# Hyena filters: output layer in two float32r passes, its input stored by step

## The chip, the cores and the metric

The kernel runs on one core of one Trainium2 chip. The metric is the device time of one launch in microseconds, as the median of several runs. The core's engines work at the same time, each through its own instruction stream in order: TensorE (PE in the profile, with its weight loads as PEld), VectorE (DVE), ScalarE (ACT), GpSimd (POOL) and SyncE (SP, which here issues nearly all DMAs).

## The reference

One encoder layer on a sequence of 2048 rows of width 1024: an input projection, a Hyena group of 512 channels beside an mLSTM group, an output projection, cross-attention, an MLP and a final norm. What the change touches is how the Hyena filters are made:

```python
def _hyena_filter_spectrum(L, w1, b1, fr1, w2, b2, fr2, w3):
    ...
    hid = jnp.sin(fr1.astype(f32) * (z @ w1.astype(f32) + b1.astype(f32)))
    hid = jnp.sin(fr2.astype(f32) * (hid @ w2.astype(f32) + b2.astype(f32)))
    filt = (hid @ w3.astype(f32)).reshape(L, HYENA_ORDER, FILTER_DIRS, D_HYENA)
    ...
    filt = filt * jnp.exp(-t * jnp.abs(deltas))[:, None, None, :]
    fwd = filt[:, :, 0]
    bwd = jnp.flip(filt[1:, :, 1], axis=0)
    two_sided = jnp.concatenate([fwd, jnp.zeros((1, HYENA_ORDER, D_HYENA), f32), bwd], axis=0)
    return jnp.fft.rfft(two_sided, axis=0)
```

There are two orders (`o`), two directions (`r`: forward, backward), 64 hidden features and 512 channels. "The output layer" is `hid @ w3`.

## The kernel before

The program is written as Python generators that yield the weight of the work they have just put down; `weave(a, b, wa, wb)` (L1594) takes turns between two of them in proportion to the weights. A scheduler then orders the instructions of each engine ahead of time by a simulated timeline, with the order of the program as priority, and adds the semaphores; tiles of one tag share a fixed number of buffers, and an instruction that needs a buffer waits until it is free.

The first stage weaves `filters()` (L158) with `sweep()` (L500), which multiplies the input projection. Each `sweep` step is 24 matmuls of `mm3` (L294 to L297): a float32 product made of three passes over operands that were cut into a high and a low part of type float32r (`split`, L299: ScalarE writes the rounded high part, VectorE subtracts to get the low one). A float32r matmul is one pass. The filters' own matmuls (L208, L212, L238, L253, L254, L284) are plain float32, each two records in the trace.

`filters()` has three parts.

- L202 to L213, four chunks of 512 positions: features, two small matmuls and two `sine` calls (L189 to L199). Both directions are computed at once, forward features on rows 0 to 63, backward ones on rows 64 to 127. The result is `hid`, 128 rows by 2048 positions.
- L244 to L264, the output loop, eight steps `j2` of two position classes `j` each (all positions congruent to `j` modulo 16) and two orders: the forward taps are a matmul of rows 0 to 63 of `hid[.., j::16]` with rows 0 to 63 of `w3` (L253), the backward taps one of rows 64 to 127 (L254). VectorE multiplies both by the decay windows (L256, L257, loaded at L224), adds them into `e[0]` (L261), GpSimd subtracts them into `e[1]` (L262). One round later (`late`) the two products with the first Fourier stage `f1` follow (L238, "fronts"), ScalarE copies them into `st` (L239), and SP stores them to the DRAM tensors `fs0` and `fs1` (L241).
- L266 to L286, 32 "blocks": load `dm` and a piece of `fs` (L268, L270), two matmuls (L284), two copies (L285), store to the DRAM tensor `hd` (L286).

All this lives in one pool, `f_sb`, with seven buffers `a` of 4 KB per partition and eight `b` of 2 KB; PSUM tiles `hy` have four banks, `mm` of the sweeps another four.

`hyena()` (L626) follows, woven with the rest of the sweeps and the natural-order products (`natural`, L593). Its middle loop (i from 0 to 15, for each order) loads per step `dm` and `em` (128 KB each), `t` from `zs` (512 KB), and four pieces of `hd` of 256 KB (L663, L664), each of 64 partitions, as the real and imaginary rows go to both halves of the partitions; it stores 512 KB to `zg`.

Of the kernel before, what the change touches and what calls it, by code (L numbers as in the profile page):

```python
# [18 lines left out]
L = 2048  # L19
D = 1024  # L20
CH = 512
# [6 lines left out]
def shape_constants():  # L28
# [39 lines left out]
    dm = np.zeros((32, 2, 64, 2, 64))  # L68
# [29 lines left out]
class Prog:  # L98
# [59 lines left out]
    def filters(self):  # L158
        nc, tc, a = self.nc, self.tc, self.a
        sd = [self.dram(f"fs{o}", (2, 128, 16, CH)) for o in range(2)]  # L160
        hd = self.dram("hd", (2, 32, 128, CH))
        with tc.tile_pool(name="f_sb", bufs=1, side="right") as sb:
            def ta(bufs=7):
                return sb.tile([128, 2, CH], F32, tag="a", name="a", bufs=bufs)

            def tb(bufs=8):
                return sb.tile([128, CH], F32, tag="b", name="b", bufs=bufs)

            w1 = sb.tile([66, 128], F32, name="w1")
            w2 = sb.tile([128, 128], F32, name="w2")  # L170
            w3 = sb.tile([128, 2, CH], F32, name="w3")
            f1 = sb.tile([128, 2, 128], F32, name="f1")
            nc.vector.memset(w1, 0.0)
            nc.vector.memset(w2, 0.0)
            nc.gpsimd.dma_start(out=w1[0:33, 0:64], in_=a["hy_filt_w1"][0])
            nc.gpsimd.dma_start(out=w1[33:66, 64:128], in_=a["hy_filt_w1"][0])
            nc.gpsimd.dma_start(out=w2[0:64, 0:64], in_=a["hy_filt_w2"][0])
# [37 lines left out]
            skip, skip2 = tb(), tb()  # L215
            for o, t in enumerate((skip, skip2)):
                nc.scalar.dma_start(out=t[0:1], in_=a["hy_skip"][:, o])
            wv = a["c_win"].rearrange("r (q j) c -> r q j c", j=16)
            def windows(j2):
                if j2 == 8:  # L220
                    return None
                w = ta(), ta()
                for r in range(2):
                    nc.sync.dma_start(out=w[r], in_=wv[r, :, 2 * j2:2 * j2 + 2])  # L224
                return w

            held = []
# [1 line left out]
            def late(f):  # L229
                if held:  # L230
                    held.pop()()
                if f is not None:
                    held.append(f)
# [7 lines left out]
                        nc.sync.dma_start(out=sd[o][p, :, js], in_=st[p])  # L241

            nxt = windows(0)
            for j2 in range(8):  # L244
                js = slice(2 * j2, 2 * j2 + 2)
                yield 14
                (wf, wb), nxt = nxt, windows(j2 + 1)
                for o in range(2):
                    st = [ta() for p in range(2)]
                    for jj in range(2):  # L250
                        j = 2 * j2 + jj
                        pf, pb = self.hy(), self.hy()
                        nc.tensor.matmul(pf, hid[0:64, j::16], w3[0:64, o], start=True, stop=True)  # L253
                        nc.tensor.matmul(pb, hid[64:128, j::16], w3[64:128, o], start=True, stop=True)  # L254
                        f, b = tb(), tb()
                        nc.vector.tensor_tensor(f, pf, wf[:, jj], ALU.mult)  # L256
                        nc.vector.tensor_tensor(b, pb, wb[:, jj], ALU.mult)  # L257
                        if j == 0:
                            nc.vector.tensor_tensor(f[0:1], f[0:1], (skip, skip2)[o][0:1], ALU.add)
                        e = [tb() for p in range(2)]  # L260
                        nc.vector.tensor_tensor(e[0], f, b, ALU.add)  # L261
                        nc.gpsimd.tensor_tensor(e[1], f, b, ALU.subtract)  # L262
                        late(lambda e=e, st=st, jj=jj, o=o, js=js: front(e, st, jj, o, js))
            late(None)  # L264
            def blocks(o, i):
                p, k = divmod(2 * i, 16)  # L266
                dm = sb.tile([128, 2, 128], F32, tag="dm", name="dm", bufs=3)
                nc.sync.dma_start(out=dm, in_=a["c_dm"][:, 2 * i:2 * i + 2])  # L268
                t = ta()
                nc.sync.dma_start(out=t, in_=sd[o][p, 8 * k:8 * k + 16].rearrange("(k r) j c -> (r j) k c", k=2))  # L270
                return dm, t

            order = [(o, i) for o in range(2) for i in range(16)]
            q = [blocks(*order[0]), blocks(*order[1])]
            for n, (o, i) in enumerate(order):
                if True:
                    yield 3.4
                    dm, t = q.pop(0)
                    if n + 2 < 32:
                        q.append(blocks(*order[n + 2]))  # L280
                    hs = ta()
                    for m in range(2):
                        pp = self.hy()
                        nc.tensor.matmul(pp, dm[:, m], t[:, m], start=True, stop=True)  # L284
                        nc.scalar.copy(hs[:, m], pp)  # L285
# [307 lines left out]
    def natural(self, hf, tiles, after=None):  # L593
        nc, a, sb = self.nc, self.a, self.isb
        xh, xl = self.xh, self.xl
        win = a["w_in"][0]
        for c2 in tiles:
            n = 256 if c2 < 3 else 272
            c0 = 2560 + 256 * c2
            wh, wl = next(self.wst)  # L600
            for t in range(8):
                if t % 4 == 0:
                    yield 11
                if t == 4 and c2 == tiles[-1] and after is not None:
                    after()
                ts = slice(128 * t, 128 * t + 128)
                r0 = 1024 * hf + 128 * t
                p = self.mm()
                for k in range(8):
                    self.mm3(p[:, :n], xh[:, k, ts], xl[:, k, ts], wh[:, k, :n], wl[:, k, :n], k == 0, k == 7)  # L610
                if self.pending:
                    self.pending.pop(0)()
                self.pop()
                so = sb.tile([128, 256], F32, tag="so", name="so", bufs=3)
                if c2 < 2:
                    nc.scalar.copy(so, p[:, :256])
                else:
                    nc.scalar.activation(so, p[:, :256], AF.Sigmoid)
                nc.sync.dma_start(out=(self.d_vd if c2 < 2 else self.d_od)[r0:r0 + 128, 256 * (c2 % 2):256 * (c2 % 2) + 256],
                                  in_=so)  # L620
                if c2 == 3:
                    sg = sb.tile([128, 16], F32, tag="sg", name="sg", bufs=2)
                    nc.vector.tensor_tensor(sg, p[:, 256:272], self.gb, ALU.add)
                    nc.sync.dma_start(out=self.d_gt[r0:r0 + 128], in_=sg)

    def hyena(self, es):  # L626
        nc, tc, a = self.nc, self.tc, self.a
        hy = self.dram("hy", (3, L, CH)).rearrange("s (q j) c -> s q j c", j=16)
        hd = self.dram("hd", (2, 32, 128, CH))
# [23 lines left out]
        def load2(o, i):  # L653
# [4 lines left out]
            nc.sync.dma_start(out=em, in_=a["c_em"][:, 2 * i:2 * i + 2])  # L658
            t, hr, hi = ta(), ta(), ta()
            nc.sync.dma_start(out=t, in_=sds[o][p, 8 * k:8 * k + 16].rearrange("(k r) j c -> (r j) k c", k=2))  # L660
            src = hd[o, 2 * i:2 * i + 2].rearrange("k (r l) c -> r l k c", r=2)
            for h in range(2):
                nc.sync.dma_start(out=hr[64 * h:64 * h + 64], in_=src[0])  # L663
                nc.sync.dma_start(out=hi[64 * h:64 * h + 64], in_=src[1])  # L664
            if i == 0:
                nc.sync.dma_start(out=hr[64:65, 0], in_=hd[o, 0, 64:65])
# [28 lines left out]
        for o in range(2):  # L695
# [16 lines left out]
            nxt = load2(o, 0)  # L712
# [899 lines left out]
def program(p):  # L1612
    with ExitStack() as ms:
        with ExitStack() as es:
# [61 lines left out]
```

## Time and profile before

| | us |
|---|---|
| median of 3 runs | 3396.99 (3387.59 to 3401.57) |
| the profiled execution | 3389.34 |
| its span | 3387.6 |
| filters' sine chunks | up to 112 |
| filters' output loop | 112 to 304 |
| filters' blocks | 304 to 463 |
| Hyena (order 0 middle loop: 520 to 720) | from 475 |

The mean granted clock of TensorE in this execution was 0.978 of full speed. In the profile a line gives engine, operation, tiles (written <- read) and shape; "idle before" is the time in which that engine stood still ahead of these instructions, with what ended it. Ends of matmuls are modelled, so that a record's length holds its passage through the array: matmuls that follow each other overlap in the records, and their cost is the distance from start to start.

### The profile page before, as it was taken

What the parts mean: (1) busy time and instruction counts of PE and PEld (TensorE: products, weight loads), DVE (VectorE), ACT (ScalarE), POOL (GpSimd) and SP (SyncE); (2) the same over time, 40 slices, a digit from 0 to 9 for tenths busy, and PEclk for the clock granted to TensorE, in tenths of its full rate; (3) what the DMA queues carried; (4) which work ended last, traced back from release to release, by engine and by line L of the source; (5) the groups of instructions that cost most, each with busy time, mean ns of one, the idle gap of its engine ahead of it and who ended that gap; (6) DMA issues with size and microseconds to landing.
All of it is one profiled execution on the core that took longest, in us unless ns stands there. A gap on an engine that the chain in (4) does not pass through costs nothing.

```text
span 3387.6 us, 46777 instructions
## 1 busy us (share of the span) xinstructions
PE 3200.0 (94%) x15671; PEld 2560.6 (76%) x15671; DVE 2084.2 (62%) x3855; ACT 1459.1 (43%) x2771; POOL 1227.3 (36%) x862
## 2 busy tenths in 40 slices
PE   6999999899899988799999999999999999999997
PEld 5656666577676877688897987788788887888876
DVE  7584324443556757787776554765854576556695
ACT  4344434442554233344344444555655543333335
POOL 2131001210122312333325012876766564434482
PEclk9999999899999989899999999999999999999998
DMA  5356888996999578856547444765654475444424
GB/s 164 115 205 206 277 288 232 258 322 254 253 242 296 178 236 277 256 162 215 187 152 265 144 134 155 224 206 184 199 171 157 148 242 174 128 140 140 128 94 159
DMA packets 480750, 674.55 MB, mean 199 GB/s; under 512 B 41739, under 2 KB 256849, under 8 KB 479485
## 3 DMA queue, kind: packets, MB, share of 16 engines
q1 hardware_dynamic: 478904, 668.70, 62.4%
q0 software_dynamic: 1600, 2.86, 0.3%
q8 instruction: 124, 2.03, 0.2%
q14 instruction: 118, 0.96, 0.1%
q10 hardware_dynamic: 4, 0.00, 0.0%
HBM read 452.23 MB, written 219.18 MB: 198 GB/s over the span
## 4 chain that ended last, share of the span: by engine, by line
PE 47%; DVE 7%; DMA 6%; issue 2%; ACT 1%; POOL 1%; SPq 0%; DVEq 0%; ACTq 0%; POOLq 0%
PE mm L297 10%; PE mm L295 10%; PE mm L296 10%; PE hy L297 5%; PE hy L296 5%; PE hy L295 5%; DVE rw L945 1%; DVE wl L301 1%; DMA rw<-rows 1%; DMA wr<-xs 1%; DVE bl L1266 1%; PE hy L1092 1%; DMA wn<-in_xa_wq_dram 1%; DMA wr<-in_ff_w_dram 0%; PE hy L972 0%
## 5 line engine op out<-in xcount | busy, mean ns | idle before, releaser
L301 DVE TENSOR_TENSOR wl<-wn,wh 128x512 fp32r<-128x512 f32 (+1 forms) x352 | 263.1, 778 | 135.0 <-ACT wh L300 134.4
L295 PE MATMUL mm<-xh,wh 128*128 128x512 f32 (+1 forms) x768 | 316.7, 413 | 10.9 <-ACT P L530 9.3
L1266 DVE TENSOR_TENSOR bl<-wr,bh 128x512 fp32r<-128x512 f32 x213 | 237.0, 1118 | 133.2 <-ACT bh L1265 131.2
L297 PE MATMUL mm<-xh,wl 128*128 128x512 f32 (+1 forms) x768 | 302.8, 395 | 3.3 <-DVE wl L301 3.3
L1265 ACT CAST ah<-w 128x512 fp32r<-128x512 f32 x284 | 176.2, 622 | 299.9 <-PE hy L296 153.7
L296 PE MATMUL mm<-xl,wh 128*128 128x512 f32 (+1 forms) x768 | 303.7, 396 | 0.2 <-DVE xr_y L150 0.2
L300 ACT CAST wh<-wn 128x512 fp32r<-128x512 f32 (+1 forms) x352 | 202.0, 618 | 229.9 <-PE mm L296 77.1
L727 POOL TENSOR_TENSOR b<-b,a 128x512 f32<-128x512 f32 x64 | 91.9, 1438 | 498.1 <-ACT b L725 201.1
L1266 DVE TENSOR_TENSOR al<-w,ah 128x512 fp32r<-128x512 f32 x236 | 224.4, 952 | 56.8 <-ACT ah L1265 56.5
L1265 ACT CAST bh<-wr 128x512 fp32r<-128x512 f32 x232 | 143.5, 621 | 241.6 <-PE mm L297 171.1
L297 PE MATMUL mm<-bh,al 128*128 128x512 f32 x576 | 225.5, 394 | 6.6 <-DVE al L1266 3.8
L295 PE MATMUL mm<-bh,ah 128*128 128x512 f32 x576 | 227.1, 394 | 0.3 <-DVE u L1391 0.2
L296 PE MATMUL mm<-bl,ah 128*128 128x512 f32 x576 | 225.8, 392 | 0.0
L295 PE MATMUL mm<-act,wh 128*128 128x512 f32 x512 | 202.0, 398 | 6.2 <-ACT wh L300 6.2
L296 PE MATMUL mm<-act,wh 128*128 128x512 f32 x512 | 202.6, 396 | 0.0
L297 PE MATMUL mm<-act,wl 128*128 128x512 f32 x512 | 201.1, 397 | 0.0
L295 PEld LDWEIGHTS mm<-xh,wh 128*128 128x128 f32 x768 | 148.2, 193 | 60.0 <-issue 18.2
L1131 POOL TENSOR_TENSOR ssum<-ssum,sq 128x512 f32<-128x512 f32 x56 | 81.3, 1451 | 284.7 <-ACT sq L1130 283.9
L297 PEld LDWEIGHTS mm<-xh,wl 128*128 128x128 f32 x768 | 147.8, 192 | 46.3 <-issue 15.8
L296 PEld LDWEIGHTS mm<-xl,wh 128*128 128x128 f32 x768 | 147.9, 193 | 45.5 <-issue 20.0
L295 PE MATMUL hy<-bh,ah 128*128 128x512 f32 x448 | 175.2, 391 | 0.0
L296 PE MATMUL hy<-bl,ah 128*128 128x512 f32 x448 | 174.6, 390 | 0.0
(373 smaller groups left out, 8911.9 us busy)
## 6 DMA issues: line engine op xcount, KB each, us to landing
wr<-hc SPq DMA_DIRECT2D x224, 256.0 KB
w<-in_ff_w_dram SPq DMA_DIRECT2D x176, 256.0 KB
a<-hd SPq DMA_DIRECT2D x128, 256.0 KB
hc<-t SPq DMA_DIRECT2D x128, 256.0 KB
wn<-in_w_in_dram SPq DMA_DIRECT2D x104, 256.0 KB
hc<-q SPq DMA_DIRECT2D x96, 256.0 KB
fs<-a SPq DMA_DIRECT2D x32, 512.0 KB
a<-fs SPq DMA_DIRECT2D x32, 512.0 KB
```

The costliest lines, as they stand in the source:

```text
L295: mm(ps, lh, rh, start=start, stop=False)
L296: mm(ps, lh, rl, start=False, stop=False)
L297: mm(ps, ll, rh, start=False, stop=stop)
L300: self.nc.scalar.copy(hi, src)
L301: self.nc.vector.tensor_tensor(lo, src, hi.bitcast(F32), ALU.subtract)
L727: nc.gpsimd.tensor_tensor(xt, xt, hi[:, m], ALU.mult)
L945: nc.vector.scalar_tensor_tensor(nm[:, h], nm[:, h], GC[:, r + h:r + h + 1], masks[d], ALU.add, ALU.min)
L1092: nc.tensor.transpose(pt[:, 128 * k:128 * k + 128], yn[:, 128 * k:128 * k + 128], self.ident)
L1131: nc.gpsimd.tensor_tensor(ssum, ssum, sq, ALU.add)
L1265: self.nc.scalar.copy(hi, src)
L1266: eng.tensor_tensor(lo, src, hi.bitcast(F32), ALU.subtract)
```

## The change

The output layer becomes float32r. `hid` is written twice, by step: `hid0` holds the high part of the forward rows on partitions 0 to 63 and their low part on 64 to 127; `hid1` the backward rows' high part on 64 to 127 and their low part on 0 to 63. `wide[r]` holds the high part of `w3[r]` on both halves, `wl` the low part (forward on 0 to 63, backward on 64 to 127). Per step, order and direction a matmul of 128 rows gives (high + low) x high, and one of 64 rows adds high x low into the same bank. The stationary operand `hid[r][:, j]` is now contiguous. Windows come one step `j` at a time with both directions in one load. The subtraction overwrites `b`. The blocks get a pool of their own, `f_sb2`. `hd` is laid out so that a row of both frequencies is contiguous, in its stores and loads. `so` of `natural` now uses the tag `st`, which the sweeps' transposed outputs and the norm's scratch also use. The weights of `weave` and the yields change (14 per two steps to 5.3 per step; 230 to 202).

```diff
-    c_win = np.stack([win, winb], 0)
+    c_win = np.stack([win.reshape(128, 16, CH), winb.reshape(128, 16, CH)], 2)
...
-        hd = self.dram("hd", (2, 32, 128, CH))
+        hd = self.dram("hd", (2, 16, 128, 2, CH))
...
-            def ta(bufs=7):
-                return sb.tile([128, 2, CH], F32, tag="a", name="a", bufs=bufs)
-
-            def tb(bufs=8):
-                return sb.tile([128, CH], F32, tag="b", name="b", bufs=bufs)
...
+            def ta():
+                return sb.tile([128, 2, CH], F32, tag="a", name="a", bufs=6)
+
+            def tb():
+                return sb.tile([128, CH], F32, tag="b", name="b", bufs=6)
+
+            ws = ta()
+            w1, w2 = ws[0:66, 0, 0:128], ws[:, 1, 0:128]
...
-            for h in range(2):
-                nc.gpsimd.dma_start(out=w3[64 * h:64 * h + 64], in_=w3v[h])
+            top, low = slice(0, 64), slice(64, 128)
+            raws = [ta() for r in range(2)]
+            for r in range(2):
+                for half in (top, low):
+                    nc.gpsimd.dma_start(out=raws[r][half], in_=w3v[r])
+            wide = [sb.tile([128, 2, CH], F32R, name=f"w3h{r}") for r in range(2)]
+            wl = sb.tile([128, 2, CH], F32R, name="w3l")
...
-            hid = sb.tile([128, L], F32, name="hid")
+            hid = [sb.tile([128, 16, 128], F32R, name=f"hid{r}") for r in range(2)]
...
-                sine(hid[:, cs], p2, 2, 3)
...
+                out = tb()
+                sine(out, p2, 2, 3)
+                src = out.rearrange("p (q j) -> p j q", j=16)
+                qs = slice(32 * c, 32 * c + 32)
+                for r, (own, other) in enumerate(((top, low), (low, top))):
+                    nc.scalar.copy(hid[r][own, :, qs], src[own])
+                    nc.vector.tensor_tensor(src[own], src[own], hid[r][own, :, qs].bitcast(F32), ALU.subtract)
+                    nc.scalar.copy(hid[r][other, :, qs], src[own])
+            for r, own in enumerate((top, low)):
+                for o in range(2):
+                    tc.keep_in_program_order(nc.scalar.copy(wide[r][:, o], raws[r][:, o]))
+                    nc.vector.tensor_tensor(wl[own, o], raws[r][own, o], wide[r][own, o].bitcast(F32), ALU.subtract)
...
+            for j in range(16):
+                jj = j % 2
+                js = slice(j - jj, j - jj + 2)
+                yield 5.3
+                cur, nxt = nxt, windows(j + 1)
+                if jj == 0:
+                    st = [[ta() for p in range(2)] for o in range(2)]
                 for o in range(2):
...
+                    taps = []
+                    for r, own in enumerate((top, low)):
+                        p = self.hy()
+                        nc.tensor.matmul(p, hid[r][:, j], wide[r][:, o], start=True, stop=False)
+                        nc.tensor.matmul(p, hid[r][own, j], wl[own, o], start=False, stop=True)
+                        t = tb()
+                        nc.vector.tensor_tensor(t, p, cur[:, r], ALU.mult)
+                        taps.append(t)
+                    f, b = taps
+                    if j == 0:
+                        skip = tb()
+                        nc.scalar.dma_start(out=skip[0:1], in_=a["hy_skip"][:, o])
+                        nc.vector.tensor_tensor(f[0:1], f[0:1], skip[0:1], ALU.add)
+                    e = tb()
+                    nc.vector.tensor_tensor(e, f, b, ALU.add)
+                    nc.gpsimd.tensor_tensor(b, f, b, ALU.subtract)
+                    late(lambda e=(e, b), st=st[o], jj=jj, o=o, js=js: front(e, st, jj, o, js))
             late(None)
+        with tc.tile_pool(name="f_sb2", bufs=1, side="right") as sb:
...
-                    nc.sync.dma_start(out=hd[o, 2 * i:2 * i + 2].rearrange("k l c -> l k c"), in_=hs)
+                nc.sync.dma_start(out=hd[o, i], in_=hs)
...
-                so = sb.tile([128, 256], F32, tag="so", name="so", bufs=3)
+                so = sb.tile([128, 512], F32, tag="st", name="st", bufs=3)[:, 0:256]
...
-            src = hd[o, 2 * i:2 * i + 2].rearrange("k (r l) c -> r l k c", r=2)
+            src = hd[o, i].rearrange("(r l) k c -> r l k c", r=2)
...
-            weave(p.filters(), s, 230, 200)
+            weave(p.filters(), s, 202, 200)
```

More of the change, by code (lines that the diff above doesn't have):

```diff
@@ L160, in filters @@
         sd = [self.dram(f"fs{o}", (2, 128, 16, CH)) for o in range(2)]
-        hd = self.dram("hd", (2, 32, 128, CH))
+        hd = self.dram("hd", (2, 16, 128, 2, CH))
         with tc.tile_pool(name="f_sb", bufs=1, side="right") as sb:
-            def ta(bufs=7):
-                return sb.tile([128, 2, CH], F32, tag="a", name="a", bufs=bufs)
-            def tb(bufs=8):
-                return sb.tile([128, CH], F32, tag="b", name="b", bufs=bufs)
-            w1 = sb.tile([66, 128], F32, name="w1")
-            w2 = sb.tile([128, 128], F32, name="w2")
-            w3 = sb.tile([128, 2, CH], F32, name="w3")
+            def ta():
[4 more added lines that the diff above has]
+            w1, w2 = ws[0:66, 0, 0:128], ws[:, 1, 0:128]
             f1 = sb.tile([128, 2, 128], F32, name="f1")
-            nc.vector.memset(w1, 0.0)
-            nc.vector.memset(w2, 0.0)
+            nc.vector.memset(ws[:, :, 0:128], 0.0)
             nc.gpsimd.dma_start(out=w1[0:33, 0:64], in_=a["hy_filt_w1"][0])
@@ L212, in filters, with windows @@
                 nc.tensor.matmul(p2, w2, hid1, start=True, stop=True)
-                sine(hid[:, cs], p2, 2, 3)
[L215 to L220, printed above, removed]
-                    return None
-                w = ta(), ta()
-                for r in range(2):
-                    nc.sync.dma_start(out=w[r], in_=wv[r, :, 2 * j2:2 * j2 + 2])
+                out = tb()
[10 more added lines that the diff above has]
+                    nc.vector.tensor_tensor(wl[own, o], raws[r][own, o], wide[r][own, o].bitcast(F32), ALU.subtract)
+            def windows(j):
+                if j == 16:
+                    return None
+                w = ta()
+                nc.sync.dma_start(out=w, in_=a["c_win"][:, j])
                 return w
@@ L243, in filters @@
             nxt = windows(0)
[L244 to L247, printed above, removed]
-                for o in range(2):
[L249 to L263, printed above, removed]
@@ new lines, in filters @@
+            st = None
+            for j in range(16):
[5 more added lines that the diff above has]
+                    st = [[ta() for p in range(2)] for o in range(2)]
+                for o in range(2):
+                    taps = []
[15 more added lines that the diff above has]
+                    late(lambda e=(e, b), st=st[o], jj=jj, o=o, js=js: front(e, st, jj, o, js))
@@ L268, in blocks @@
                 nc.sync.dma_start(out=dm, in_=a["c_dm"][:, 2 * i:2 * i + 2])
-                t = ta()
+                t = sb.tile([128, 2, CH], F32, tag="a", name="a", bufs=8)
                 nc.sync.dma_start(out=t, in_=sd[o][p, 8 * k:8 * k + 16].rearrange("(k r) j c -> (r j) k c", k=2))
@@ L275, in filters @@
             for n, (o, i) in enumerate(order):
[L276 to L285, printed above, removed]
-                    nc.sync.dma_start(out=hd[o, 2 * i:2 * i + 2].rearrange("k l c -> l k c"), in_=hs)
+                yield 3.4
+                dm, t = q.pop(0)
+                if n + 2 < 32:
+                    q.append(blocks(*order[n + 2]))
+                hs = sb.tile([128, 2, CH], F32, tag="a", name="a", bufs=8)
+                for m in range(2):
+                    pp = self.hy()
+                    nc.tensor.matmul(pp, dm[:, m], t[:, m], start=True, stop=True)
+                    nc.scalar.copy(hs[:, m], pp)
+                nc.sync.dma_start(out=hd[o, i], in_=hs)
     def column(self, ap, n, name):
@@ L628, in hyena @@
         hy = self.dram("hy", (3, L, CH)).rearrange("s (q j) c -> s q j c", j=16)
-        hd = self.dram("hd", (2, 32, 128, CH))
+        hd = self.dram("hd", (2, 16, 128, 2, CH))
         yh = self.dram("yh", (L, CH)).rearrange("(q j) c -> q j c", j=16)
@@ L665, in load2 @@
             if i == 0:
-                nc.sync.dma_start(out=hr[64:65, 0], in_=hd[o, 0, 64:65])
+                nc.sync.dma_start(out=hr[64:65, 0], in_=hd[o, 0, 64:65, 0])
                 nc.vector.memset(hi[0:1, 0], 0.0)
```

## The prediction, made before the changed kernel ran

> **What bounds the kernel now.** I read the page's totals first, then the busy time by stage, then the order of instructions on TensorE inside the stage that the change rewrites.
>
> ```profile
> span 3387.6 us, 46777 instructions
> PE 3200.0 (94%) x15671; PEld 2560.6 (76%) x15671; DVE 2084.2 (62%) x3855; ACT 1459.1 (43%) x2771; POOL 1227.3 (36%) x862
> ```
>
> ```profile
> 20.00:47.00 27.00, 17.07 (x64) 12.85 (x65) 22.49 (x83) 14.23 (x30) 2.81 (x5) 0.96 0.80 251
> ...
> 112.00:304.00 192.00, 190.19 (x650) 109.33 (x649) 137.50 (x273) 77.37 (x147) 56.71 (x31) 1.00 0.49 169
> ...
> 463.00:475.00 12.00, 10.28 (x51) 8.41 (x50) 5.29 (x8) 5.01 (x8) 0.59 (x1) 1.00 0.69 227
> ```
>
> A row of the windows gives its length, then busy time of PE, PEld, DVE, ACT and POOL, the granted clock, the DMA share and GB/s. The filters' output loop runs from 112 to 304 us: TensorE is busy 190.2 of 192 us at full clock, DVE 137.5. So in that stage time is TensorE time, and the question is how much of it the old output layer takes. Its matmuls are L253 and L254, which read `hid` on rows 0–63 and 64–127. The first row below is both lines together, the second L254 alone (windows from 0 to 304 us).
>
> ```profile
> sum 304.00, PE 56.27 PEld 24.55 ACT 2.53; mean PE 11.25 PEld 4.91 ACT 0.51
> ```
>
> ```profile
> sum 304.00, PE 38.94 PEld 16.42; mean PE 7.79 PEld 3.28
> ```
>
> Two times 38.94 is 77.9, yet together they keep TensorE busy for only 56.3 us: 21.6 us of it two matmuls ran at once. One float32 matmul of 64 rows is two records, 1.23 us; 21.6 / 1.23 makes some 18 of the 32 pairs that run side by side, and 14 that don't. The timeline shows one of each.
>
> ```profile
> 205.21 0.40 PE L295 MATMUL mm<-xh,wh 128*128 128x512 f32 x1
> ...
> 205.45 0.40 PE L296 MATMUL mm<-xl,wh 128*128 128x512 f32 x1
> 205.77 0.29 PEld L253 LDWEIGHTS hy<-w,hid 64*128 64x128 f32 x1 [0.37 <-issue]
> 205.77 0.80 PE L253 MATMUL hy<-w,hid 64*128 64x512 f32 x1
> ...
> 205.78 0.80 PE L254 MATMUL hy<-w,hid 64*128 64x512 f32 x1
> ...
> 206.41 0.59 PE L253 MATMUL hy<-w,hid 64*128 64x512 f32 x1
> ...
> 206.94 0.19 PEld L297 LDWEIGHTS mm<-xh,wl 128*128 128x128 f32 x1 [0.65 <-issue]
> 206.94 0.51 PE L297 MATMUL mm<-xh,wl 128*128 128x512 f32 x1
> ...
> 207.28 1.02 PE L238 MATMUL hy<-b,f 128*128 128x512 f32 x2
> ```
>
> ```profile
> 250.39 0.40 PE L296 MATMUL mm<-xl,wh 128*128 128x512 f32 x1
> 250.72 1.23 PE L254 MATMUL hy<-w,hid 64*128 64x512 f32 x2
> 251.88 0.50 PE L297 MATMUL mm<-xh,wl 128*128 128x512 f32 x1
> ```
>
> Read starts, not durations. A single pass of 128 rows follows the one before after 0.23 to 0.24 us (205.21 to 205.45). Before the 64-row pair the step is 0.32 (205.45 to 205.77), 0.09 more; the pair takes 1.17 (205.77 to 206.94); the first 128-row pass after it takes 0.34 (206.94 to 207.28), 0.11 more. Thus each change between 64 and 128 rows costs time: the old pass drains, and the new weights are loaded in the open.
>
> **The output layer on TensorE.** Before: a side-by-side pair costs 1.17 + 0.09 + 0.11 = 1.37 us, a lone one 1.16 (250.72 to 251.88) + 0.20 = 1.36, so a split pair 2.72. 18 x 1.37 + 14 x 2.72 = 62.7 us.
> After: each (step, order) has four single passes in the sequence 128 rows, 64 rows, 128 rows, 64 rows; the two 64-row passes are never neighbours, so none runs beside another, and each makes two changes of height. A lone 64-row pass: 0.23 + 0.09 drain ahead + 0.11 weight load in the open (stationary operand now contiguous: I take the 0.19 us load of L297, not the strided 0.29) + 0.09 drain behind (as the 0.09 ahead) + 0.11 for the next load = 0.63. Two of these and two plain passes at 0.23 are 1.72; times 32 is 55.0. **Term: -7 us** (62.7 - 55.0, rounded towards zero). No row has a 64-row pass of this type. Ends: if height changes cost nothing, 4 x 0.23 x 32 = 29.4, -33; if the load stays as slow as the strided one, 0.10 x 64 more, -1. I take -7, since its rows are this array in this stage.
> By the Trainium skill, TensorEngine Tiling (Array Packing), Key Properties, changing the tiling mode drains TensorE; that speaks against a layer that alternates heights, and by it the sum would be the same -7, while a count of passes alone would give -33. The trace agrees: the 0.09 us steps above.
>
> **Splitting `hid` and `w3`.** It adds 16 ScalarE copies and 8 VectorE subtractions of 64 x 512, and 4 of each for the weights.
>
> ```profile
> 80.00:112.00 32.00, 31.96 (x152) 25.51 (x151) 24.05 (x42) 12.35 (x20) 0.00 (x0) 1.00 0.27 75
> ```
>
> ```profile
> L301 DVE TENSOR_TENSOR wl<-wn,wh 128x512 fp32r<-128x512 f32 (+1 forms) x352 | 263.1, 778 | 135.0 <-ACT wh L300 134.4
> L300 ACT CAST wh<-wn 128x512 fp32r<-128x512 f32 (+1 forms) x352 | 202.0, 618 | 229.9 <-PE mm L296 77.1
> ```
>
> 20 x 0.62 = 12.4 us of ACT and 12 x 0.78 = 9.4 of DVE, over the stretch that ends at 112 us, where DVE has 8 of 32 us free and TensorE is full of sweep matmuls. **Term: 0**; without that cover the last split and the weights (about 0.62 + 0.78 + 0.62 + 4 x 0.78 = 5 us) delay the loop, so 0 to +5. Six `b` buffers at 3 tiles a round still leave two rounds in flight, as eight at 4 did: 0.
>
> **The start.** In the old kernel four window loads and three `dm` loads are issued ahead of the last two x tiles.
>
> ```profile
> 11.43 7.51 SPq L224 DMA_DIRECT2D a<-in_c_win_dram  x4
> ...
> 19.43 2.15 SPq L268 DMA_DIRECT2D dm<-in_c_dm_dram  x3
> ...
> 22.23 1.50 SPq L398 DMA_DIRECT2D xn<-in_x_dram  x2
> ...
> 34.12 0.63 ACT L406 ACTIVATE junk<-xn 128x512 f32<-128x512 f32 x1 [4.11 <-DMA xn<-in_x_dram]
> ```
>
> Those are 4 x 512 + 3 x 128 KB. Of six `a` buffers three now hold weights, so two windows (1 MB) can go early, and `dm` sits in the second pool: 1.4 MB less, against 0.5 MB more of `w3` on POOL's queue. 0.9 MB at the 251 GB/s of 20 to 47 us is 3.6 us, and ScalarE waited 4.1 us for that x tile. **Term: -3** (0 to -4).
>
> **The seam.** Blocks now live in a second pool over the first one's memory.
>
> ```profile
> 301.51 1.48 SPq L270 DMA_DIRECT2D a<-fs  x3
> ...
> 309.66 1.54 SPq L241 DMA_DIRECT2D fs<-a  x2
> ```
>
> ```profile
> 313.88 1.88 PE L284 MATMUL hy<-a,dm 128*128 128x512 f32 x4
> ```
>
> Block loads ran ahead at 301.5, before the last `fs` stores were issued at 309.7; they must now wait for these to land. L284 starts some 5 us later than 313.9, with sweep matmuls as cover. At the like seam before Hyena (463 to 475 us) TensorE lost 12.0 - 10.3 = 1.7 us. **Term: +2** (0 to +5).
>
> **`hd` in 4 KB pieces.** Its stores and loads halve their pieces' number.
>
> ```profile
> 316.00:365.00 49.00, 49.00 (x203) 34.42 (x203) 12.10 (x18) 21.59 (x38) 0.00 (x0) 1.00 0.85 276
> ```
>
> ```profile
> 520.00:720.00 200.00, 180.25 (x740) 125.92 (x739) 95.63 (x165) 105.25 (x173) 44.09 (x32) 0.96 0.98 256
> 720.00:760.00 40.00, 38.46 (x207) 27.96 (x208) 12.27 (x22) 5.49 (x12) 0.00 (x0) 1.00 0.95 355
> ```
>
> ```profile
> DVE b L726 <- DMA a<-hd: 24.7, 7, 6.1
> ```
>
> Stores lie in the block stage, where TensorE is full: 0. Loads lie in 520 to 720, where DMA is the bound (0.98) and TensorE idles 19.8 us. Per full DMA share this stage moves 256 / 0.98 = 261 GB/s, the block stage, whose `fs` loads and `hd` stores are also in 2 KB pieces but on 128 partitions, 325, and 720 to 760, mostly 4 KB pieces, 374. So piece size is worth about 13%, and the rest is something the edit keeps (`hd` is loaded on 64 partitions at a time). Of each step's 2.25 MB, 1 MB is `hd`: 0.44 x 13% of 200 us is 11 us of DMA time. VectorE's waits of 24.7 us for `hd` are few and long, so I let 4 of it reach TensorE. **Term: -4** (0 to -20).
> By the Trainium skill, SBUF — State Buffer, Door 1, a transfer to 64 partitions reaches half of the 16 ports whatever its pieces; by it this term would be near 0, and the lower rate above agrees with it.
>
> **Small edits.** The two skip loads move on ScalarE's queue from behind the sines into step 0, where two VectorE additions wait for them, `so` shares three `st` buffers, each `fs` buffer is rewritten a step later instead of rotating among seven. **Term: +2** (0 to +6: ScalarE's idle before L239 for `fs` was 2.5 us in all).
>
> **Sum:** -7 + 0 - 3 + 2 - 4 + 2 = -10 us. The profiled execution took 3389.3 us (span 3387.6), hence 3379 for one like it; the median of the runs is 3397.0, so I predict 3387.
>
> **Rivals.**
> (a) *Height changes are free for single passes*: -33 instead of -7, so 3361. For it: nothing but the count of passes; against: the 0.32 and 0.34 steps happen between single passes of this very type and a 64-row load.
> (b) *Whole pieces free Hyena's loads*: `hd` at 374 GB/s would save more DMA time than TensorE idles, so all 19.8 us return: -26 in all, 3371. Against: the 325 GB/s of 2 KB pieces.
> (c) *Slower: POOL behind VectorE.* The subtraction now overwrites `b`, so it waits for the addition that it used to run beside, and the second front matmul waits for it; behind that on TensorE's queue stand the next pair and the sweeps.
>
> ```profile
> L261 DVE TENSOR_TENSOR b<-b 128x512 f32<-128x512 f32 x32 | 25.3, 790 | 0.7
> ```
>
> ```profile
> L262 POOL TENSOR_TENSOR b<-b 128x512 f32<-128x512 f32 x32 | 58.5, 1828 | 223.3 <-DVE b L257 187.1 <-DVE xr_y L155 8.7 <-DVE xr_t L153 8.0
> ```
>
> ```profile
> POOL b L262: 3.2, 8
> ```
>
> The last row is what L238's weight loads waited for POOL. Exposed every time it costs 32 x 0.79 = 25 us: 3387 + 25 = 3412. It decides from 13 of the 32 (10 / 0.79). For it: POOL's 1.83 us and a DVE that is busy 72% of the stage; against: after the second tap's matmul TensorE has fronts and another pair, 2 x 1.72 + 0.86 = 4.3 us, ahead of that front, and the chain needs 0.7 + 0.79 + 1.83 = 3.3.
>
> **Chances.** Forecast 0.47, (a) 0.11, (b) 0.14, (c) 0.28. The forecast's own range is 3372 to 3402. 0.5% (17 us) is about what a measurement here can tell from no change; the three runs before span 14. Faster than 3380: all of (a), 0.11 of (b), 0.28 of the forecast, 0.35. Slower than 3414: a little over half of (c) and 0.03 of the forecast, 0.17. The rest, 0.48, is no change. The range takes (a)'s and (c)'s values in: 3360 to 3416.
>
> **What would show it.** Right: 64-row records of about 0.6 us from step to step, alone; the output loop's lines some 55 us; x tiles 6 and 7 issued before 20 us; DMA still near 0.98 from 520 to 720. Wrong: 64-row passes at 0.23 steps (a), TensorE full in Hyena's second phase (b), L238 waiting 15 us or more for POOL (c). A different order of the sweeps on TensorE would make all terms wrong together.

## The result, and the profile after

The changed kernel took 3402.90 us (median of 19 runs), the kernel before 3391.19 us (19 runs) beside it. The ratio is 1.0032, 95% interval 1.0020 to 1.0045: about 11 us slower, inside the half per cent that the prediction called no change. The predicted 3387 was 10 us below its starting point. The time lay inside the predicted range, but the sign was wrong.

The page's totals of the changed kernel; this execution took 3394.59 us:

```profile
span 3392.9 us, 46847 instructions
...
PE 3204.0 (94%) x15671; PEld 2566.7 (76%) x15671; DVE 2091.3 (62%) x3866; ACT 1481.0 (44%) x2791; POOL 1206.0 (36%) x864
```

Busy time by stage, same kernel (length, then PE, PEld, DVE, ACT, POOL, the granted clock, DMA share, GB/s):

```profile
20.00:47.00 27.00, 14.90 (x50) 10.52 (x50) 20.40 (x74) 13.07 (x28) 3.97 (x7) 1.00 0.80 231
...
112.00:304.00 192.00, 190.76 (x702) 116.38 (x701) 138.97 (x292) 88.43 (x161) 40.58 (x30) 0.99 0.52 173
...
463.00:475.00 12.00, 12.00 (x51) 8.82 (x51) 5.35 (x9) 4.43 (x7) 0.59 (x1) 1.00 0.82 259
520.00:720.00 200.00, 184.09 (x768) 129.83 (x767) 93.81 (x142) 100.37 (x165) 43.44 (x32) 0.97 0.97 264
```

TensorE has as many matmuls as before. The start lost 2.2 us of TensorE's work (14.90 against 17.07). The output loop's stage is as full as before; its 702 records where 650 stood prove little by themselves, since the mix of passes changed. From 463 to 475 us TensorE no longer idles (12.00 us busy against 10.28).

Around one output pair, TensorE's timeline in the changed kernel reads:

```profile
207.19 0.39 PE L310 MATMUL mm<-xh,wh 128*128 128x512 f32 x1
207.42 0.40 PE L265 MATMUL hy<-w3h,hid 128*128 128x512 f32 x1
207.75 0.49 PE L266 MATMUL hy<-w3l,hid 64*128 64x512 f32 x1
208.17 0.50 PE L311 MATMUL mm<-xl,wh 128*128 128x512 f32 x1
208.51 0.39 PE L312 MATMUL mm<-xh,wl 128*128 128x512 f32 x1
```

From start to start: 0.23 us into the 128-row pass, 0.33 from it to the 64-row pass, 0.42 to the next 128-row pass, 0.34 to the one after. The pair costs 0.33 + 0.42 + 0.11 = 0.86 us, as predicted (0.63 + 0.23). The 64-row passes stand alone, and the steps around them are longer than 0.23 us, so rival (a) is out.

Rival (c) needed TensorE to wait 15 us for POOL. The groups of the subtraction (L277) and the addition (L276), and then what the weight loads of the fronts waited for in the stretch 100 to 320 us:

```profile
L277 POOL TENSOR_TENSOR b<-b 128x512 f32<-128x512 f32 x32 | 43.1, 1348 | 248.7 <-DVE b L276 202.8 <-DVE xr_t L154 7.5 <-DVE P L543 7.0
L276 DVE TENSOR_TENSOR b<-b 128x512 f32<-128x512 f32 x32 | 21.9, 684 | 0.6
```

```profile
PEld hy L247 <- POOL b L277: 1.7, 3, 1.2
PEld hy L247 <- DVE b L276: 1.4, 1, 1.4
```

The two operations now run one after the other, as (c) said, but in the mean each is shorter: 1348 ns instead of 1828, 684 instead of 790. The chain of both is 2.03 us where the prediction counted 0.79 + 1.83 = 2.6. TensorE waited 1.7 us for the subtraction in all, far from 15, so rival (c) is out too.

At the start the timeline of the changed kernel shows what went wrong:

```profile
12.37 4.55 SPq L413 DMA_DIRECT2D xn<-in_x_dram  x2
...
17.23 1.80 SPq L233 DMA_DIRECT2D a<-in_c_win_dram  x2
...
21.19 0.61 POOL L187 DMA_DIRECT2D a<-in_hy_filt_w_dram  x1
...
22.96 13.50 SPq L342 DMA_DIRECT2D wn<-in_w_in_dram  x4
23.21 1.79 POOL L187 DMA_DIRECT2D a<-in_hy_filt_w_dram  x3 [1.41 <-DMA par<-in_hy_filt_b_dram]
...
34.72 1.14 ACT L315 CAST wh<-wn 128x512 fp32r<-128x512 f32 x2 [6.51 <-DMA wn<-in_w_in_dram]
...
35.77 0.58 ACT L315 CAST xh<-mm 128x512 fp32r<-128x512 f32 x1
...
36.40 0.79 PE L310 MATMUL mm<-xh,wh 128*128 128x512 f32 x1 [6.25 <-ACT xh L315]
```

The same place in the kernel before:

```profile
23.09 0.61 POOL L186 DMA_DIRECT2D w<-in_hy_filt_w_dram  x1 [0.99 <-DMA par<-in_hy_filt_b_dram]
...
24.86 7.08 SPq L327 DMA_DIRECT2D wn<-in_w_in_dram  x3
...
30.96 1.42 PE L295 MATMUL mm<-xh,wh 128*128 128x512 f32 x1
```

The two x tiles (`xn`) and only two windows go early, as predicted. But four pieces of `w3` instead of two now share the DMA engines with the sweep's first weights `wn`. ScalarE waits 6.51 us for these weights, the cast of `x` that stands behind it in order waits too, and the first sweep matmul starts at 36.40 instead of 30.96 us.

### The profile page after: what moved, and what is told of

Read it like the earlier page. It is cut to its first block, busy times and chain, and to the rows that moved or that the text cites. A ratio compares the mean times of both kernels' runs of the same rounds, so it can differ in the third digit from the quotient of the medians.

```text
span 3392.9 us, 46847 instructions
## 1 busy us (share of the span) xinstructions
PE 3204.0 (94%) x15671; PEld 2566.7 (76%) x15671; DVE 2091.3 (62%) x3866; ACT 1481.0 (44%) x2791; POOL 1206.0 (36%) x864
## 3 DMA queue, kind: packets, MB, share of 16 engines
q8 instruction: 124, 2.03, 0.3%
## 4 chain that ended last, share of the span: by engine, by line
PE 47%; DVE 6%; DMA 5%; issue 2%; ACT 1%; POOL 1%; SPq 0%; DVEq 0%; ACTq 0%; POOLq 0%
PE mm L312 10%; PE mm L311 10%; PE mm L310 10%; PE hy L312 5%; PE hy L310 5%; PE hy L311 5%; DMA rw<-rows 1%; DVE wl L316 1%; DVE rw L960 1%; PE hy L1107 1%; DMA wn<-in_w_out_dram 1%; DVE bl L1281 1%; DVE al L1281 0%; DMA wn<-in_xa_wq_dram 0%; PE hy L1203 0%
```

## The experiments

Ratios are against the kernel before on the same chip. Times from different chips are not compared, since the kernel before itself had medians from 3384.31 to 3398.38 us on them. Two quantities are taken from the records of each trace: the start of TensorE's n-th matmul (counted from 0; all kernels have 15671), and the distances from start to start of all output and front matmuls, with what the first sweep pass behind them takes over 0.232 us.

```
start of the n-th matmul, us; the first column is before_same, the others: difference from it
n      before_same  before  before_seam  changed  w3_late  both   best_so_st  best
300        97.2      +0.1      +1.1        +6.9     +1.6    +1.4     +1.0     +0.7
1200      347.6       0.0      +1.1        -2.8     -5.5    -5.0    -18.3    -19.5
2400      669.9     +15.0      +4.9        +3.8     -4.0    -2.3    -13.0    -18.3
4800     1173.4      +2.3      +0.3        +2.6     -4.9    -7.6    -17.0    -25.1
7800     1696.7      -1.1      +1.9        +3.3     -7.5    -5.6    -12.0    -30.7
15600    3355.0      -0.6      +1.6        +4.3     -7.3    -4.8    -12.6    -29.8

start-to-start time of the 256 output and front records (us):
before 115.4   changed 112.2   both 111.8   rows128 99.1   best 96.5
```

"changed" is the execution `after_timed` in the first table and the profiled one in the second.

`before_again`, the same program once more, stands at +0.4, +0.3, +5.7, +2.1, +6.1 and +8.0 us in these six rows. So three executions of the kernel before agree within 0.4 us up to the 1200th matmul, and from the 2400th on a difference of 8 us in one trace says little.

**The two kernels again**, one execution each on one chip:

> The kernel before, unchanged, profiled a second time. All theories: 3382 to 3402 us. Read against the first profile it says how far one stretch of the program moves between two executions; if the stretch from 1130 to 1550 us moves by 5 us or more on its own, a loss of that size there in one profile of the changed kernel is not yet a loss.

> The changed kernel, unchanged, profiled a second time. All theories: 3393 to 3417 us. Theory A (loss after Hyena, from 1130 us on): it is 5 to 9 us ahead of the kernel before at 750 us and behind it at 1800 us, as in the first profile. Theory B (loss in the filters' own stage): it is behind at 750 us.

Measured 3397.88 and 3402.59 us. The difference of 5 us has the measured sign; single runs tell no more. The kernel before does move by itself: from 1130 to 1550 us its first profile gains about 4 us on `before_same` and `before_again` loses about 3. At 750 us `after_again` is behind `before_again` (2763 matmuls started against 2781), where the first profiles had the changed kernel ahead (2771 against 2733), so theory A was not confirmed.

**`so` out of the shared buffers**, in the changed kernel (`sop` is a pool opened after the filters), and the opposite edit in the kernel before:

```diff
-                so = sb.tile([128, 512], F32, tag="st", name="st", bufs=3)[:, 0:256]
+                so = self.sop.tile([128, 256], F32, tag="so", name="so", bufs=3)
...
```

> The changed kernel with the natural products' output tiles in three buffers of their own again (a pool opened after the filters), all else as in the change. Theory A1 (natural's copies wait for the sweeps' transposed stores in the shared ring): 6 to 12 us faster than the changed kernel, so 3391 to 3397, ratio to before 1.000 to 1.002; ScalarE's waits for the kn stores ahead of the sigmoid copies vanish. Theory A2 (another order of instructions after Hyena, not the ring): within 4 us of the changed kernel.

> The kernel before with one edit: the natural products' output tiles share the three st buffers. Theory A1 (the shared ring costs after Hyena): 4 to 9 us slower than before (ratio 1.001 to 1.003), lost between 1130 and 1300 us. Theory A2 (the order of instructions there, not the ring): ratio 0.999 to 1.001.

Ratios: `so_own` 1.0017 (1.0002 to 1.0032), `before_so_st` 1.0033 (1.0018 to 1.0047). Sharing `st` alone costs the kernel before 11 us. ScalarE's waits between 1060 and 1460 us (us in total, times, longest), first in the kernel before, then in `before_so_st`:

```profile
ACT so L616 <- DMA vd<-so: 18.5, 5, 5.3
```

```profile
ACT st L618 <- DMA kn<-st: 8.3, 2, 6.4
...
ACT L618 <- DMA kn<-st: 7.6, 1, 7.6
```

The copies to `so` now wait for stores of `kn`, which leave from the same three buffers; their wait for their own stores is gone. These waits for stores do not grow in sum (15.9 us against 18.5), so they show the new coupling but not where the 11 us are lost. With its own buffers back the changed kernel is 0.13% below its 1.0030, about 4 us, and the intervals overlap; the waits for `kn` stores at the `so` copies are gone, as expected.

**The height changes removed**: the second pass takes 128 rows, which adds the low part of `hid` times the low part of the other direction's `w3`.

```diff
-                        nc.tensor.matmul(p, hid[r][own, j], wl[own, o], start=False, stop=True)
+                        nc.tensor.matmul(p, hid[r][:, j], wl[:, o], start=False, stop=True)
```

> [...] If a change of height costs what the prediction says (0.39 us for each 64-row pass), the output loop loses 64 x 0.39 = 25 us and the kernel is 20 to 27 us faster than the changed one (3376 to 3383, ratio 0.995 to 0.998). If it costs nothing, no difference beyond 4 us.

The ratio is 0.9977 (0.9964 to 0.9990): against the changed kernel's 1.0030 that is 18 us, give or take 6, not 25. TensorE's timeline:

```profile
203.27 0.40 PE L310 MATMUL mm<-xh,wh 128*128 128x512 f32 x1
203.50 0.40 PE L265 MATMUL hy<-w3h,hid 128*128 128x512 f32 x1
203.74 0.39 PE L266 MATMUL hy<-w3l,hid 128*128 128x512 f32 x1
203.96 0.40 PE L311 MATMUL mm<-xl,wh 128*128 128x512 f32 x1
204.20 0.39 PE L312 MATMUL mm<-xh,wl 128*128 128x512 f32 x1
```

Every step is 0.22 to 0.24 us: the price of a lone 64-row pass, 0.39 us over a plain one, is entirely the change of height. Yet over the whole loop the start-to-start time falls by 112.2 - 99.1 = 13 us, not 64 x 0.39 = 25.

**The `w3` loads held back** until the first sine chunk, by a one-column copy into their buffers; the four loads at the top of `filters()` go:

```diff
...
+                if c == 0:
+                    for r in range(2):
+                        nc.vector.tensor_copy(raws[r][:, 0, 0:1], src[:, 0, 0:1])
+                        for half in (top, low):
+                            nc.gpsimd.dma_start(out=raws[r][half], in_=w3v[r])
```

> The changed kernel, with the four loads of w3 held back until the first sine chunk is done (a one-column copy into their tiles goes first). Theory C (the start is late because w3, now loaded twice and in 64-partition pieces, shares the DMA engines from 28 to 34 us with the sweeps' first weights): the first sweep matmul moves from 36.4 to about 31 us, and the kernel is 4 to 7 us faster than the changed one (3391 to 3399 beside a before of 3392 to 3398). Rival D (the start is late because of the order on ScalarE, casts of weights ahead of the cast of x, whatever the DMA does): first matmul still after 34 us, no difference beyond 3 us.

The ratio is 0.9995 (0.9980 to 1.0010), 0.35% or 12 us under the changed kernel's 1.0030. Its timeline:

```profile
23.31 11.01 SPq L344 DMA_DIRECT2D wn<-in_w_in_dram  x8
...
34.11 0.79 PE L312 MATMUL mm<-xh,wh 128*128 128x512 f32 x1
...
54.48 2.38 POOL L225 DMA_DIRECT2D a<-in_hy_filt_w_dram  x4 [32.61 <-DVE a L223]
```

With the loads moved to 54 us the first sweep matmul comes at 34.11 instead of 36.40 us, and the 300th is 1.6 us late instead of 6.9. The trace gives 5 us to these loads, the timed runs 12, with an interval of some 6 to either side. The gain is theory C's. But the first sweep matmul came after 34 us, as rival D said, and not near 31. It does so in `before_seam` below too (34.54 us), which loads `w3` as the kernel before does and is only 1.1 us late at the 300th matmul: some 3 of the 5.4 us by which the first matmul moved are not the `w3` loads' doing, and cost little.

**`hd` in 4 KB pieces alone**, in the kernel before:

```diff
-        hd = self.dram("hd", (2, 32, 128, CH))
+        hd = self.dram("hd", (2, 16, 128, 2, CH))
...
```

> The kernel before with one edit: hd laid out so that both frequencies of a row are contiguous, stores and loads. The prediction's term: 4 us faster (0 to 20; ratio 0.999 if 4). Rival (64 partitions set the rate, not the piece): no difference, ratio 0.9995 to 1.0005, and DMA share times rate from 520 to 720 us unchanged at about 260 GB/s for a full share.

Ratio 0.9988 (0.9977 to 0.9999): 4 us (0 to 8), the predicted size, though the rival's 0.9995 is inside the interval. Its row of the stage that should gain:

```profile
520.00:720.00 200.00, 185.83 (x811) 132.73 (x810) 100.41 (x173) 109.21 (x181) 42.88 (x32) 0.99 0.97 269
```

Per full DMA share that is 269 / 0.97 = 277 GB/s. It is more than the 261 of the profile on which the prediction rests, but `before_same`, with 2 KB pieces, has 270 / 0.97 = 278 (its row stands in the last section). The traces show no faster transfers.

**The fixes together**, without and with the second pass of 128 rows, and the changed kernel timed beside the first:

> The changed kernel with w3 held back and own buffers for the natural products' output, the 64-row passes kept. If these two are all that the prediction missed, what is left is its own sum of the output layer, hd and the seam: -7 - 4 + 2 and small edits, 5 to 13 us below before, ratio 0.996 to 0.9985; the memory projection's first transposes come 52 us after the scans' first end columns (59 to 60 with the shared ring). If something else still costs, ratio 0.999 or above.

> The changed kernel itself, timed beside the one above on the same chip: 1.002 to 1.0045 of before as in its first measurement. If it comes out at 1.000 or below here, the loss depends on the chip and the sums against it above have to be widened.

> The changed kernel with three edits: second pass on 128 rows, w3 held back, own buffers for the natural products' output. If the three effects add (18 us for the rows, 5 for the start, 5 for the ring against the changed kernel): 3402 - 28 = 3374 beside a before of 3392 to 3398, ratio 0.993 to 0.996. If TensorE isn't the bound of the output loop any more, the rows give no more than they gave alone: ratio 0.9955 to 0.998.

`both` measured 0.9997 (0.9986 to 1.0008), the changed kernel 1.0030 (1.0019 to 1.0042), `best` 0.9941 (0.9924 to 0.9958), 3366.71 us where the kernel before had 3385.88. `best` beats both kernels. But `both` did not reach the 0.996 to 0.9985 that my sum gave: some 8 us were still missing. Four more runs searched for them.

> The kernel before itself, once more: a control, and a profile of it on the same chip as the run beside it. Theory A (an execution differs from the next one by some us, and chips by more, but the medians of one chip agree): ratio 1.000 with an interval of about +-0.0012, and a span some us off the two spans of this kernel that are there, 3387.6 and 3396.2. Theory B (the differences between profiles of this kernel are a property of the run's place in the call): ratio off 1 by over 0.1%.

> The changed kernel with late w3 loads and so in buffers of its own (`both`, 0.9997 of before), and hd back in 2 KB pieces. The terms left in `both` were layer -7, hd -4, seam +2 and small edits, some -8 us or 0.9976, and it measured -1. Theory A (hd in 4 KB is worth the 2 to 4 us here that it was worth alone in the kernel before; what is missing lies in the layer, the seam or the later order): 1.0003 to 1.001. Theory B (in the new order hd's loads are hidden or blocked by something else, and its gain is what is missing): 0.9997 again, within 0.0005. In the traces: A shows the stretch of Hyena's first middle loop some 4 us longer than in `both`, B the same length.

`before_same` is the kernel before against itself: 1.0002 (0.9988 to 1.0015), as a control should be. `both_hd_old` is `both` with `hd` in 2 KB pieces: 1.0008 (0.9996 to 1.0020). That is theory A in size (0.0011 above `both`), but the intervals overlap, and in the traces the stage 520 to 720 us is alike, as B said: TensorE busy 185.40 us at 269 GB/s, in `both` 184.65 at 270. So these runs don't settle whether `hd` keeps its 4 us.

**`so` in the faster kernel, and the seam alone.** `best_so_st` is `best` with `so` back in the `st` buffers; `before_seam` is the kernel before with

```diff
+        with tc.tile_pool(name="f_sb2", bufs=1, side="right") as sb:
             def blocks(o, i):
...
-                t = ta()
+                t = sb.tile([128, 2, CH], F32, tag="a", name="a", bufs=8)
...
```

The three `dm` loads thereby leave the early queue too, as in the changed kernel, so that the start changes with the seam.

> The changed kernel with late w3 loads and second passes of 128 rows (so low x low of the other direction is added), and so left in the shared st buffers: `best` (0.9941 of before) with only so put back. Theory A (sharing st costs what it cost in the kernel before, 11 us): 0.9973. Theory B (in the changed order the wait for st is hidden or made up, as `both` against w3_late says, 0.9997 and 0.9995): 0.9941 to 0.995. Half of it would be 0.9957. In the trace both expect ScalarE's waits for st at the so copies and the memory projection's transposes some 58 us after the scans' first matmul; A expects the lateness to be still there at the end, B to be gone by the 5400th matmul.

> The kernel before, with its blocks in a pool of their own over the first one's memory (eight a buffers), and nothing else: the seam alone. Theory A (the prediction's term): +2 us (0 to +5), 1.0006 (1.000 to 1.0015), the blocks' first matmul some 5 us later than at 313.9 us. Theory B (the seam is where the missing 5 to 10 us lie): 1.0015 to 1.003, and TensorE behind by that much at the 1500th matmul. Theory C (it gains, since more buffers let block loads run ahead): 0.999.

`best_so_st`: 0.9959 (0.9946 to 0.9971), half of what A expected, some 6 us over `best`, with intervals that overlap. ScalarE's waits there between 1060 and 1460 us are those of `before_so_st`:

```profile
ACT st L635 <- DMA kn<-st: 8.4, 2, 6.1
...
ACT L635 <- DMA kn<-st: 7.6, 1, 7.6
```

`before_seam`: 1.0019 (1.0005 to 1.0033), 6 us, B by time. Its SP issues around the seam:

```profile
310.73 1.54 SPq L241 DMA_DIRECT2D fs<-a  x2
...
316.04 0.33 SPq L269 DMA_DIRECT2D dm<-in_c_dm_dram  x1
316.43 0.43 SPq L271 DMA_DIRECT2D a<-fs  x1
```

and TensorE's first block matmul:

```profile
322.11 1.88 PE L285 MATMUL hy<-a,dm 128*128 128x512 f32 x4
```

The block loads wait for the last `fs` stores, as predicted (SP's `dm` loads wait 2.7 us for them), and the blocks' first matmul starts at 322.1 instead of 313.9 us, 8 us later where 5 had been said. But TensorE isn't behind by that at the 1500th matmul, as B said it would be: sweep matmuls cover the gap (the 1200th is 1.1 us late, and so was the 300th). The 6 us that the timed runs show come later, where in this one execution I can't place them.

**How far each kernel was at 463 us**, from the traces above. All output, front and block matmuls and the same transposes have then started in each of the kernels below; they differ in the sweep passes alone, of which one takes 0.26 us from start to start (223.0 us / 858 in `before_same`).

```
sweep passes started by 463 us
kernel before (three traces), before_so_st, before_hd_new   852 to 859
changed kernel (three traces), so_own                       842 to 854
before_seam                                                 853
w3_late                                                     881
both, both_hd_old                                           878 and 879
```

So the changed kernel is about 2 us behind the kernel before there (849 passes in the mean against 856), `before_seam` level with it, and `both` 6 us ahead.

## Why the prediction was wrong

**The start: a wrong sign.** The step "0.9 MB at the 251 GB/s of 20 to 47 us is 3.6 us … Term: -3 (0 to -4)" is the one that failed first. It weighed bytes taken from the early queue against bytes added, and took the x tiles as what ends the wait. The x tiles did come earlier, and were no longer the limit: the weights `wn` were, at 28 to 35 us, and the extra `w3` loads run just there. Each is a load into 64 partitions, and the two halves of a buffer are loaded from the same source. The changed kernel is 6.9 us late at the 300th matmul in place of 3 early. Holding the `w3` loads back takes away 5 us of it by that row, some 8 by the sweep passes at 463 us (881 against 842 to 854) and some 12 by the timed runs. The profile before had a row of the kind: at 42.11 us ScalarE waits 2.92 us for a tile `wn`, and a cast of `x` stands behind it, since the engine takes its instructions in order.

By the Trainium skill, SBUF — State Buffer, Door 1, a load into 64 partitions reaches half of the 16 ports, so that each of the four loads by itself would be slower than its bytes into 128 rows. The late `wn` does not tell this from the doubled bytes: no run here loaded the same `w3` bytes on 128 partitions.

**`so` in the `st` buffers: a term lost among the small edits.** "`so` shares three `st` buffers" was one of three edits priced together at +2 (0 to +6), by ScalarE's waits for `fs`, another tile in another stage. Alone it cost 11 us in the kernel before; in `best` it was 6 and in the changed kernel 4, neither clear of the noise, and `both` against `w3_late` shows none (0.9997 and 0.9995). So I take about 5 us here, an estimate; only its direction in the kernel before is certain. The row that should have been read is what ScalarE's copies to `so` waited for (18.5 us above): their own stores already, so the ring was short of buffers before `kn` joined it. The other two small edits were not tested alone.

**The output layer: right in the piece, half in its own records.** "32 x 1.72 = 55.0 … Term: -7". Every step of it was met, 0.86 us for a pair between sweep passes. But in the changed kernel only 16 of the 64 second passes stand ahead of a sweep pass, and only 9 of the first passes behind one; the others have another output pass, a front or a transpose beside them. Over all 256 records of outputs and fronts the gain is 115.4 - 112.2 = 3 us. In the same way the height changes were worth 13 to 15 us of the loop (112.2 - 99.1, 111.8 - 96.5) where 25 had been expected. A price taken between sweep passes was multiplied by all pairs; how much each other neighbourhood takes off it was not resolved. The old side was read loosely too: by their starts 15 of the 32 old pairs ran side by side, not 18, with which the same sum gives 66.8 - 55.0, or -12.

**The seam: covered, as forecast.** "Term: +2 (0 to +5)" named the right mechanism. In `before_seam` the blocks start 8 us later and at 463 us nothing of it is left (853 passes). Yet that kernel takes 6 us more (2 to 11) when timed, so this edit costs something behind 463 us that the prediction had not looked for.

**`hd`: the size met, by luck.** The term was -4 because "I let 4 of it reach TensorE"; measured were -4 alone (0 to -8). Its mechanism, faster transfers in 4 KB pieces, is not seen in the traces (277 GB/s against 278).

**Right:** the split at 0 (the output loop's stage stays full); rivals (a), (b) and (c) all out, (b) by `before_hd_new` and by the 520 to 720 row above, where TensorE still idles 15.9 us. In the chances, 0.35 comes out only if 0.28 is read as a share of the forecast's 0.47 and 0.11 as a chance of its own.

**What the terms add up to, and what stays open.** Up to 463 us the forecast had -7 (layer) - 3 (start) + 2 (seam) = -8 us, and the passes give +2; with the `w3` loads held back it had -5, and `both` gives -6. So ahead of 463 us the start alone failed, while layer and seam came out together. Behind 463 us, `hd` at -4 and `so` at +5 would make the changed kernel 2 - 4 + 5 = +3, where it measured +10 and +11, and `both` -6 - 4 = -10, where it measured -1 (-5 to +3). With the 6 us of `before_seam`, each of these three kernels loses 5 to 9 us behind 463 us that no term accounts for. What they share is the blocks' pool of their own. That it is the cause is a guess: no run shows how it would cost time there, and two traces of one program differ by as much. A lead of TensorE could also be lost where DMA is the bound (share 0.97 from 520 to 720 us), but `before_seam` had none to lose. The new weights of `weave`, in the other two, were not tested alone either. This part of the slowdown stays open.

## What to carry to other kernels

At the start of a kernel, ask of each load which tile the first matmul will wait for, and what shares the DMA engines with that tile then; counting bytes in the queue misses it. Price each "small" edit that makes two kinds of work share buffers by itself, from the waits of the engine that writes them. And read a step price from all the neighbourhoods in which it will occur, not from the cleanest one; where it is the height of the array that changes, filling the idle rows with a product of two low parts took 18 us off this kernel. When a sum fails, count the work done at the end of each stage: that says on which side of it the time was lost.

## What was not expected of the hardware

The same program differs from execution to execution in its DMA-bound stretches. The stage 520 to 720 us of the kernel before, in `before_same`:

```profile
520.00:720.00 200.00, 187.03 (x809) 133.42 (x808) 100.99 (x173) 109.43 (x181) 42.89 (x32) 0.98 0.97 270
```

TensorE did 809 matmuls there, where the profile on which the prediction rests has 740 (180.25 us busy, 256 GB/s); by the 2400th matmul the two were 15.0 us apart, and by the 4800th 2.3. So the 19.8 us of idle TensorE that rival (b) and the `hd` term were built on were partly that execution's own.

VectorE's addition and GpSimd's subtraction of the same two tiles took longer side by side than one after the other: 790 and 1828 ns in the mean against 684 and 1348. The price falls on GpSimd: its median goes from 1780 to 1282 ns, while VectorE's is 692 and 683, and its higher mean comes from three of the 32 additions, of 1.76 to 1.78 us. The changed subtraction also overwrites one of its inputs, and no run separates that. By the Trainium skill, GPSIMD Engine Reference, Specifications, the two engines share their SBUF interfaces and contend when a VectorE instruction has two SBUF inputs; these rows agree in direction.
